# RWKV-7 state update: the decayed old state added by VectorE instead of accumulated on TensorE

## The chip, the cores and the metric

One core of a Trainium2 chip runs the whole block. Its engines are named as in the profile: PE is TensorE (PEld its weight loads), DVE VectorE, ACT ScalarE, POOL GpSimd, SP the queue of SyncE. The metric is the device time of one execution in microseconds; the time before is the median of 3 runs.

## The reference

A hybrid block on 512 tokens of width 1024: an RWKV-7 time mix beside a Conformer convolution (31 taps), a gated merge and a feed-forward part, all in float32. What the change touches is the recurrence of the time mix, for each of 16 heads with a 64 x 64 state S:

```
def step(S, inp):
    r_t, w_t, k_t, v_t, a_t, b_t = inp
    sa = einsum('bhvk,bhk->bhv', S, a_t)
    S = S * w_t[..., None, :] + sa[..., None] * b_t[..., None, :] + v_t[..., None] * k_t[..., None, :]
    y = einsum('bhvk,bhk->bhv', S, r_t)
    return S, y
```

## The kernel before

The activations lie transposed: 8 channel tiles of 128 channels (two heads each) by 512 tokens. The dense products run as three passes each on float32r halves (`acc3`: high by high, high by low, low by high); in the middle part of the program their weights are streamed by GpSimd's DMA queue (`wload`: `wh` as loaded, `wl` made by ScalarE and an accumulating second DMA).

The recurrence runs in 8 chunks of 64 tokens. For each channel tile `ct`, `prep` makes the decays and keys, `solve` inverts a unit triangular matrix per chunk on VectorE and TensorE, `values` makes the values, and `chain` (line 956) carries the state from chunk to chunk; `finish` normalises, and `taps` runs the convolution of that tile on VectorE as 31 long operations. In `chain`, each chunk `c` does this, every product into one PSUM tile `zt`:

- `zt[:, 0:2]`: the queries and keys of the chunk (`AR`) with the state `SV[c]` (line 978), copied by ScalarE to `zs` (981)
- `zt[:, 5:7]`: the inverse `pb` (the buffer `Pbd`) with `zs` (982), copied by ScalarE to `UV` (984)
- `zt[:, 3:5]`: for c > 0 the product of the unit matrix with the old state `SV[c]`, started (988), and the update, `bkT` with `UV[c]`, accumulated onto it (990)
- two ScalarE instructions, one per head, scale each half of `zt[:, 3:5]` by the decay of the chunk, `dL[:, c]`, and write it as `SV[c + 1]` (993)

```
PE.matmul(zt[:, 3:5, :], lhsT=ident, rhs=SV[:, c, :, :],
          start=True, stop=False)
PE.matmul(zt[:, 3:5, :], lhsT=bkT[:, c, :], rhs=UV[:, c, :, :],
          start=c == 0, stop=True)
```

The chains of the 8 channel tiles follow each other. Beside them TensorE works on dense tiles, VectorE on taps, the next tile's solve and the preparation of the one after, ScalarE on copies and activations. The order in which all this stands on each engine is set when the program is built: `Sched` keeps, per engine, queues of recorded instructions with estimated durations (`times`), and issues, engine by engine, the ready instruction of lowest priority number (0 for `chain`, 1 for loads, 2 for `prep` and `values`, 3 for `solve` and `finish`, 4 for dense products, 5 for `taps`). The order written in this way is fixed on the chip; an instruction that has to wait holds all that stands behind it on its engine. Recorded instructions carry the line of the helper that issues them, so nearly all rows say L300 (in `issue`) or L225 (in `call`), and are told apart by their tiles.

Of the kernel before, what the change touches and what calls it, by code (L numbers as in the profile page):

```python
# [9 lines left out]
F32 = mybir.dt.float32  # L10
F32R = mybir.dt.float32r
I32 = mybir.dt.int32
AF = mybir.ActivationFunctionType
ALU = mybir.AluOpType
# [3 lines left out]
P = 128  # L18
# [4 lines left out]
L = 64  # L23
# [58 lines left out]
def tile_hybrid_block(ctx, tc, xT, cst, prm, dwp, wl1, w2g, w_in, w_ro, w_co, w_o,  # L82
# [296 lines left out]
    V, G, S = Engine("DVE", nc.vector), Engine("POOL", nc.gpsimd), Engine("ACT", nc.scalar)  # L379
    PE, SY = Engine("PE", nc.tensor), Engine("SP", nc.sync)  # L380

    def pool(stack, name, bufs, **k):
        return Pool(stack.enter_context(tc.tile_pool(name=name, bufs=bufs, **k)), bufs)
# [5 lines left out]
    sp = pool(ctx, "sp", 2)  # L389
# [16 lines left out]
    ident = cs[:, C_ID:C_ID + P]  # L406
# [23 lines left out]
    E, O = slice(0, 64), slice(64, 128)  # L430
# [134 lines left out]
    for k in range(NT):  # L565
        if k == WK:
# [4 lines left out]
                               op0=ALU.mult, op1=ALU.subtract)  # L571
# [11 lines left out]
    def normed():  # L583
        for k in range(NT):
# [7 lines left out]
                    op0=ALU.mult, op1=ALU.add)  # L592
# [3 lines left out]
                    op0=ALU.mult, op1=ALU.add)  # L596
# [147 lines left out]
    def once(fn):  # L744
        fn()
        yield from ()
# [209 lines left out]
    def chain(ct):  # L956
        s_ = st[ct]
        if ct:
            yield ("chain", ct - 1)
        yield ("val", ct)  # L960
        yield ("solve", ct)
        AR, GR, UV, SV, pb, bkT, dL = (s_[n] for n in ("AR", "GR", "UV", "SV", "pb", "bkT", "dL"))
        yp = None

        def outputs(cs_):
            for c in cs_:
                if c > 0:
                    for par, R in ((0, E), (1, O)):
                        PE.matmul(yp[R, c, :], lhsT=SV[R, c, par, :], rhs=AR[R, c, 2, :],
                                  start=c == 1, stop=False, skip_group_check=True)  # L970
            for c in cs_:
                for par, R in ((0, E), (1, O)):
                    PE.matmul(yp[R, c, :], lhsT=UV[:, c, par, :], rhs=GR[:, c, par, :],
                              start=False, stop=True, skip_group_check=True)

        for c in range(NCH):
            zt = pc.tile([P, 7, L], F32, tag="ch", name="zt")
            PE.matmul(zt[:, 0:2, :], lhsT=AR[:, c, 0:2, :], rhs=SV[:, c, :, :],
                      start=True, stop=True)
            zs = sp.tile([P, 2, L], F32, tag="zs", name="zs")  # L980
            S.activation(out=zs, in_=zt[:, 0:2, :], func=AF.Copy)
            PE.matmul(zt[:, 5:7, :], lhsT=pb[:, c, :], rhs=zs, start=True, stop=True)
            for par, R in ((0, E), (1, O)):
                S.activation(out=UV[R, c, par, :], in_=zt[R, 5 + par, :], func=AF.Copy)
            if c < NCH - 1:

                if c > 0:
                    PE.matmul(zt[:, 3:5, :], lhsT=ident, rhs=SV[:, c, :, :],
                              start=True, stop=False)
                PE.matmul(zt[:, 3:5, :], lhsT=bkT[:, c, :], rhs=UV[:, c, :, :],  # L990
                          start=c == 0, stop=True)
                for par, R in ((0, E), (1, O)):
                    S.activation(out=SV[R, c + 1, par, :], in_=zt[R, 3 + par, :], func=AF.Identity,
                                 scale=dL[R, c:c + 1])
            if c == NCH // 2 - 1:
                yp = s_["yp"] = py.tile([P, NCH, L], F32, tag="y", name="yp")
                outputs(range(0, NCH // 2))
        outputs(range(NCH // 2, NCH))
        sc.post(("chain", ct))
        sc.spawn(once(lambda: finish(ct)), 3)  # L1000
# [130 lines left out]
    for ct in range(NT):  # L1131
        for g_, pri in ((prep, 2), (values, 2), (chain, 0), (taps, 5)):
            sc.spawn(g_(ct), pri)
# [242 lines left out]
    for h in range(2):  # L1376
        c = HALF[h]
# [83 lines left out]
```

## Time and profile before

| | before |
|---|---|
| median of 3 runs | 1114.42 us (1114.17 to 1115.25) |
| profiled execution, its own time | 1110.63 us |
| its span | 1108.9 us |
| TensorE busy | 1061.3 us (96%) |
| VectorE busy | 731.5 us (66%) |
| ScalarE busy | 568.2 us (51%) |
| GpSimd busy | 103.8 us (9%) |

The span is the time from the first to the last instruction; some 1.7 us lie around it. Busy shares are means over stages with different limits. Rows of the groups view give the busy time, the mean of one instruction in ns, and the idle time of the engine just before the group with what ended it; a row of a tile gives the minimum, median and maximum. A TensorE product of float32 tiles is recorded as two passes, so 48 products stand as 96.

### The profile page before, as it was taken

Reading aid. Unit: us, or ns where it says so; the run is one execution under the profiler, and the core shown is the slowest. Engines: PE = TensorE matmul, PEld = TensorE weight load, DVE = VectorE, ACT = ScalarE, POOL = GpSimd, SP = SyncE. Lnnn points to the kernel's source line nnn. Section 1 sums busy time; section 2 is a strip of 40 time slices with the busy share of each in tenths; the row PEclk is TensorE's granted clock in tenths of the full one; section 3 lists DMA queues with packets and bytes.
Section 4 is the critical chain, followed back from the end, with each engine's and each line's share of the span. In section 5 each row is a group of like instructions: output and inputs, shape, how many; then the busy total and the mean of one; then the engine's idle time right before and its main releaser. Section 6 shows DMA issues by size and latency. Waiting matters only on the chain.

```text
span 1108.9 us, 18596 instructions
## 1 busy us (share of the span) xinstructions
PE 1061.3 (96%) x7066; PEld 860.2 (78%) x7066; DVE 731.5 (66%) x1511; ACT 568.2 (51%) x1197; POOL 103.8 (9%) x172
## 2 busy tenths in 40 slices
PE   7799999999899999989999999999999999999996
PEld 5577787877787777768788888998888888888885
DVE  5878899899898999998553366365444444433324
ACT  5556666777777777555572235344333333323321
POOL 0003322211313222010000000000000000000000
PEclk9899999999899999999999999999999999999998
DMA  6115745434546454144232236102223222333312
GB/s 240 46 40 119 145 98 122 82 70 95 104 98 122 102 114 101 33 86 152 77 105 96 87 104 204 62 1 81 93 94 95 95 95 95 91 100 115 105 48 76
DMA packets 68872, 107.74 MB, mean 97 GB/s; under 512 B 15152, under 2 KB 20656, under 8 KB 68784
## 3 DMA queue, kind: packets, MB, share of 16 engines
q1 hardware_dynamic: 48912, 70.38, 20.2%
q0 software_dynamic: 19872, 36.18, 16.2%
q8 instruction: 56, 0.92, 0.3%
q14 instruction: 32, 0.26, 0.1%
HBM read 102.34 MB, written 2.10 MB: 94 GB/s over the span
## 4 chain that ended last, share of the span: by engine, by line
PE 83%; DVE 6%; ACT 4%; issue 1%; DMA 0%; DVEq 0%; ACTq 0%
PE dn L225 34%; PE dn L300 29%; PE zt L300 5%; PE psf L225 2%; PE wo L225 2%; PE yp L300 2%; PE gps L300 1%; ACT Mt L300 1%; PE lora L300 1%; DVE AR L300 1%; DVE GR L300 1%; DVE cacc L300 1%; DVE cpad L300 1%; PE ssy L300 1%; PE psn L225 1%
## 5 line engine op out<-in xcount | busy, mean ns | idle before, releaser
L225 ACT ACTIVATE wh<-wf 128x512 fp32r<-128x512 f32 x140 | 86.7, 619 | 219.2 <-PE dn L225 209.3
L225 DVE TENSOR_TENSOR wl<-wf,wh 128x512 fp32r<-128x512 f32 x140 | 94.4, 675 | 125.2 <-ACT wh L225 125.0
L300 PE MATMUL dn<-HH,wh 128*128 128x512 f32 x408 | 168.8, 414 | 0.0
L300 PE MATMUL dn<-HH,wl 128*128 128x512 f32 x408 | 168.1, 412 | 0.0
L300 PE MATMUL dn<-HL,wh 128*128 128x512 f32 x408 | 167.4, 410 | 0.0
L225 PE MATMUL dn<-FHL,wh 128*128 128x512 f32 x320 | 127.7, 399 | 0.0
L225 PE MATMUL dn<-FHH,wh 128*128 128x512 f32 x320 | 126.2, 394 | 0.0
L225 PE MATMUL dn<-FHH,wl 128*128 128x512 f32 x320 | 125.4, 392 | 0.0
L225 PE MATMUL dn<-FH,wh 128*128 128x512 f32 (+1 forms) x332 | 101.3, 388 | 0.0
L300 PEld LDWEIGHTS dn<-HH,wl 128*128 128x128 f32 x408 | 78.0, 191 | 14.4 <-issue 0.5
L300 PEld LDWEIGHTS dn<-HH,wh 128*128 128x128 f32 x408 | 77.8, 191 | 14.6 <-issue 0.7
L300 PEld LDWEIGHTS dn<-HL,wh 128*128 128x128 f32 x408 | 77.7, 190 | 14.6 <-issue 0.5
L300 ACT ACTIVATE wh<-wf 128x512 fp32r<-128x512 f32 x69 | 42.9, 627 | 78.5 <-PE dn L300 71.2
L300 DVE SCALAR_TENSOR_TENSOR cacc<-ca,dw,cacc 128x512 f32<-128x512 f32 x105 | 78.1, 744 | 0.0
L300 POOL DMA_DIRECT2D wl<-in_w_in_dram x69 | 60.4, 886 | 180.8 <-ACT wl L300 149.0
L300 DVE SCALAR_TENSOR_TENSOR cpad<-ca,dw,cpad 128x512 f32<-128x512 f32 x98 | 73.0, 745 | 0.1
L300 DVE TENSOR_TENSOR wl<-wf,wh 128x512 fp32r<-128x512 f32 x69 | 47.3, 688 | 38.6 <-ACT wh L300 38.6
L225 PEld LDWEIGHTS dn<-FH,wh 128*128 128x128 f32 x332 | 61.5, 188 | 13.9
L225 PEld LDWEIGHTS dn<-FHH,wh 128*128 128x128 f32 x320 | 60.1, 188 | 15.7
L225 PEld LDWEIGHTS dn<-FHH,wl 128*128 128x128 f32 x320 | 60.1, 188 | 14.3
L225 PEld LDWEIGHTS dn<-FHL,wh 128*128 128x128 f32 x320 | 60.1, 188 | 13.6
L225 PE MATMUL dn<-FH,wl 128*128 128x512 f32 (+1 forms) x166 | 64.0, 385 | 0.0
(306 smaller groups left out, 2101.6 us busy)
## 6 DMA issues: line engine op xcount, KB each, us to landing
wh<-in_w_in_dram POOLq DMA_DIRECT2D x69, 256.0 KB, 3.8
wl<-in_w_in_dram POOLq DMA_DIRECT2D x69, 256.0 KB, 4.4
wf<-in_w_gt_dram SPq DMA_DIRECT2D x44, 256.0 KB, 2.6
wf<-in_w_up_dram SPq DMA_DIRECT2D x44, 256.0 KB, 2.6
wf<-in_w_in_dram SPq DMA_DIRECT2D x43, 256.0 KB, 2.8
wf<-in_w_dn_dram SPq DMA_DIRECT2D x40, 256.0 KB, 2.7
wf<-in_w_ro_dram SPq DMA_DIRECT2D x16, 256.0 KB, 2.5
wf<-in_w_co_dram SPq DMA_DIRECT2D x16, 256.0 KB, 2.6
```

The lines of the kernel that those rows point to most:

```text
L225: return fn(*a, **k)
L300: i = fn(*a, **k)
```

## The change

The product with the unit matrix is left out. In its place, for c > 0, GpSimd multiplies each head's half of the old state with the decay into a new buffer `dS` (two in turn), and VectorE takes the update from PSUM, scales it by the same decay and adds `dS`, one instruction per head. For c = 0 the old ScalarE instructions stay.

```
             if c < NCH - 1:
 
                 if c > 0:
-                    PE.matmul(zt[:, 3:5, :], lhsT=ident, rhs=SV[:, c, :, :],
-                              start=True, stop=False)
+                    dS = sp.tile([P, L], F32, tag="dS", name="dS")
+                    for par, R in ((0, E), (1, O)):
+                        G.tensor_scalar(out=dS[R], in0=SV[R, c, par, :], scalar1=dL[R, c:c + 1],
+                                        scalar2=None, op0=ALU.mult)
                 PE.matmul(zt[:, 3:5, :], lhsT=bkT[:, c, :], rhs=UV[:, c, :, :],
-                          start=c == 0, stop=True)
+                          start=True, stop=True)
                 for par, R in ((0, E), (1, O)):
-                    S.activation(out=SV[R, c + 1, par, :], in_=zt[R, 3 + par, :], func=AF.Identity,
-                                 scale=dL[R, c:c + 1])
+                    if c > 0:
+                        V.scalar_tensor_tensor(out=SV[R, c + 1, par, :], in0=zt[R, 3 + par, :],
+                                               scalar=dL[R, c:c + 1], in1=dS[R], op0=ALU.mult,
+                                               op1=ALU.add)
+                    else:
+                        S.activation(out=SV[R, c + 1, par, :], in_=zt[R, 3 + par, :],
+                                     func=AF.Identity, scale=dL[R, c:c + 1])
```

Since `Sched` sees other instructions, it also writes another order on every engine. Three places of it follow.

TensorE, channel tile 0, before: chunk 1 from the product with the unit matrix to the first product of chunk 2 (`dn` are passes of dense tiles, `cs` holds the unit matrix).

```order
L300 MATMUL zt<-SV,cs 128x128
L300 MATMUL zt<-UV,bkT 128x128
L300 MATMUL dn<-HH,wl 128x512
L300 MATMUL dn<-HH,wh 128x512
L300 MATMUL dn<-HL,wh 128x512
L300 MATMUL dn<-HH,wl 128x512
L300 MATMUL dn<-HH,wh 128x512
L300 MATMUL dn<-HL,wh 128x512
L300 MATMUL zt<-SV,AR 128x128
```

And the same place in the changed program:

```order
L300 MATMUL zt<-UV,bkT 128x128
L300 MATMUL dn<-HH,wl 128x512
L300 MATMUL dn<-HH,wh 128x512
L300 MATMUL dn<-HL,wh 128x512
L300 MATMUL zt<-SV,AR 128x128
```

The product with the unit matrix is gone, and three dense passes instead of six stand between the update's product and the first product of the next chunk.

VectorE in the changed program, around the first update of channel tile 0 (`tt` and `Ps` belong to the solve of channel tile 1, `ca` to a convolution's input).

```order
L300 TENSOR_TENSOR tt<-Mo,Ps 128x24
L300 TENSOR_TENSOR Ps<-Ps,tt 128x2x3x4
L300 SCALAR_TENSOR_TENSOR SV<-zt,dL,dS 64x64 x2
L300 SCALAR_TENSOR_TENSOR ca<-th,dn 128x512
L300 TENSOR_TENSOR tt<-Mo,Ps 128x16
L300 TENSOR_TENSOR Ps<-Ps,tt 128x2x2x4
L300 TENSOR_TENSOR tt<-Mo,Ps 128x8
```

Before, the same operations of the solve stood here without the update. The updates of one tile's state now stand among the solve and the preparation of the following tiles, and each waits for the other in this order.

GpSimd in the changed program, at the first copies of channel tile 0.

```order
L300 DMA wh<-in_w_in_dram 128x512 x3
L300 DMA wl<-in_w_in_dram 128x512
L300 ISA
L300 TENSOR_SCALAR dS<-SV,dL 64x64 x2
L300 DMA wl<-in_w_in_dram 128x512
L300 DMA wh<-in_w_in_dram 128x512
L300 TENSOR_SCALAR dS<-SV,dL 64x64 x2
L300 DMA wl<-in_w_in_dram 128x512
L300 TENSOR_SCALAR dS<-SV,dL 64x64 x2
```

Before, only the DMA issues stood here. The copies stand between them, two per chunk, and the row ISA, a reload of GpSimd's code library, stands once, ahead of the first.

## Rows read from the trace of the kernel before

**Rows 1.** The page's head: span; busy time of each engine (share), instructions

```profile
span 1108.9 us, 18596 instructions
...
PE 1061.3 (96%) x7066; PEld 860.2 (78%) x7066; DVE 731.5 (66%) x1511; ACT 568.2 (51%) x1197; POOL 103.8 (9%) x172
```

**Rows 2.** Busy us (instructions) by stretch, then TensorE's clock, DMA share, GB/s

```profile
140.00:500.00 360.00, 342.60 (x3497) 273.53 (x3496) 329.16 (x792) 256.19 (x664) 82.10 (x130) 0.98 0.46 94
460.00:500.00 40.00, 33.71 (x268) 25.90 (x269) 37.13 (x67) 26.41 (x74) 5.22 (x6) 0.96 0.35 68
500.00:700.00 200.00, 199.07 (x874) 160.80 (x873) 113.99 (x187) 96.11 (x156) 0.00 (x0) 1.00 0.37 120
```

**Rows 3.** Who waited for whom, 140 to 500 us, PE and POOL: us, times, longest

```profile
PE zt L300 <- ACT SV L300: 3.7, 5, 0.9
PE zt L300 <- ACT zs L300: 2.6, 6, 0.6
...
POOL wl L300 <- ACT wl L300: 133.9, 26, 26.4
```

**Rows 4.** Tile `zt` (minimum/median/maximum ns), then groups by shape (busy us, mean ns)

```profile
L300 ACT ACTIVATE SV<-zt,dL x112: 291/309/312, 144.8 to 496.1; 64x64 f32<-64x64 f32 x112
...
L300 PE MATMUL zt<-SV,cs 128*128 128x128 f32 x96 | 19.9, 289 | 0.5 <-ACT UV L300 0.5
```

**Rows 5.** Timeline (start us, us), TensorE's weight loads around one unit-matrix product

```profile
304.58 0.19 PEld L300 LDWEIGHTS dn<-HH,wl 128*128 128x128 f32 x1
304.81 0.41 PEld L300 LDWEIGHTS zt<-SV,cs 128*128 128x128 f32 x2
305.14 0.30 PEld L300 LDWEIGHTS zt<-UV,bkT 128*128 128x128 f32 x2
305.37 0.19 PEld L300 LDWEIGHTS dn<-HH,wh 128*128 128x128 f32 x1
305.48 0.19 PEld L300 LDWEIGHTS dn<-HL,wh 128*128 128x128 f32 x1
```

**Rows 6.** VectorE's groups: tap, PSUM operand, short operation; then a timeline of taps

```profile
L300 DVE SCALAR_TENSOR_TENSOR cpad<-ca,dw,cpad 128x512 f32<-128x512 f32 x98 | 73.0, 745 | 0.1
...
L300 DVE TENSOR_TENSOR AR<-gps,cs 64x256 f32<-64x256 f32 x32 | 13.4, 419 | 10.3 <-ACT Mt L300 6.7 <-PE gps L300 3.3
...
L300 DVE SCALAR_TENSOR_TENSOR rw<-rt,ry 128x8 f32<-128x8 f32 x48 | 8.0, 166 | 1.5
...
281.95 0.75 DVE L300 SCALAR_TENSOR_TENSOR cacc<-ca,dw,cacc 128x512 f32<-128x512 f32 x1
282.61 0.75 DVE L300 SCALAR_TENSOR_TENSOR cpad<-ca,dw,cpad 128x512 f32<-128x512 f32 x1
```

**Rows 7.** Timeline at two updates of channel tile 0: ScalarE, then VectorE

```profile
148.54 0.62 ACT L300 ACTIVATE SV<-zt,dL 64x64 f32<-64x64 f32 x2
...
152.69 0.63 ACT L300 ACTIVATE SV<-zt,dL 64x64 f32<-64x64 f32 x2 [0.25 <-PE zt L300]
...
148.49 0.18 DVE L300 TENSOR_TENSOR Ps<-Ps,tt 128x24 f32<-128x24 f32 x1
```

**Rows 8.** GpSimd's groups (busy us, mean ns, idle before); then tile `SV`

```profile
L300 POOL DMA_DIRECT2D wl<-in_w_in_dram x69 | 60.4, 886 | 180.8 <-ACT wl L300 149.0 <-PE zt L300 13.3 <-ACT zs L300 13.1
L300 POOL DMA_DIRECT2D wh<-in_w_in_dram x69 | 41.8, 610 | 110.0 <-PE dn L300 100.1 <-PE zt L300 8.8 <-issue 0.8
...
L300 POOL MEMSET SV<- x16: 144/146/527, 67.7 to 430.1; 64x64 f32 x16
```

**Rows 9.** Tile `wl`, the streamed weights, from issue to landing

```profile
DMA to landing us min/median/max: 3.7/4.4/6.4
```

**Rows 10.** Timeline of GpSimd: ahead of the first updates, and at two memsets

```profile
145.06 0.88 POOL L300 DMA_DIRECT2D wl<-in_w_in_dram  x1 [0.20 <-issue]
...
298.55 0.90 POOL L300 DMA_DIRECT2D wl<-in_w_in_dram  x1 [0.84 <-ACT mu_v L300]
299.10 0.71 POOL L300 MEMSET SV<- 64x64 f32 x2
```

## The prediction

> **What bounds the kernel now.** I read the page's header and busy shares first, then busy time by stretch, then who waits for whom inside the stretch that the change touches, then single steps.
>
> The profiled execution took 1110.63 us (span 1108.9 and 1.7 around it). TensorE is busy 96% of the span, VectorE 66%, ScalarE 51%, GpSimd 9% [rows 1]. The state updates run from 144.8 to 496.1 us [rows 4], so the stage to look at is 140 to 500 us. There TensorE is busy 342.6 of 360 us, VectorE 329.2 (91%), ScalarE 256.2 (71%), GpSimd 82.1, and after it, to 700 us, TensorE is full but for 1 us [rows 2]. So TensorE sets the time, with VectorE close behind it. TensorE's largest waits there are a few us each: 3.7 us in 5 places for the old update on ScalarE, 2.6 us for `zs`, and none for a streamed weight [rows 3]. A microsecond of work taken off TensorE should therefore mostly come off the time, as long as no new wait takes its place. The exception is the end of the stage: from 460 to 500 us TensorE is busy 33.7 of 40 us and VectorE 37.1 [rows 2].
>
> **The unit-matrix product, removed.** There are 48 (8 channel tiles, chunks 1 to 6), recorded as 96 passes of 0.289 us mean [rows 4]. Passes overlap, so this duration is not their price; the pitch is. In the weight loads from 304.81 to 305.48 us stand two passes of this product, two of the product with `bkT`, and one dense pass; two dense loads alone stand 0.23 apart [rows 5]. So (305.48 - 304.81 - 0.23) / 4 = 0.11 us a pass, and 96 x 0.11 = 10.6 us. Six of the 48 products are those of the last channel tile, in the stretch where TensorE has idle time; I count seven eighths: **-9.3 us**, with -10.6 as the far end.
>
> **The scaled copy out of PSUM, moved from ScalarE to VectorE.** ScalarE loses 96 of its 112 `SV` instructions of 0.309 us [rows 4], some 30 us, at a place where it is 71% busy: nothing by itself. VectorE gains 96. It has no such shape now. Its fixed part is 0.166 us (128x8) and 256 columns from PSUM cost 0.419 [rows 6], so 64 columns are about 0.166 + 56 x 0.253 / 248 = 0.22 us, estimated from these two. A pair is then 0.4 to 0.45 us where ScalarE's pair spans 0.62 [rows 7]: up to 0.2 us shorter a step. TensorE waits only 3.7 us in all for that pair [rows 3], so the gain lies between 0 and 3.7 us; I take 0, for the reason that follows.
>
> **The new wait on VectorE.** The update now stands in VectorE's fixed order among the conv taps, the solve of the next channel tile and the preparation of the one after. It can find in front of it one tap of 0.745 us [rows 6], and what stands behind a late update is the next chunk's first product on TensorE, and all of TensorE's queue behind it. Ends: 0 if the dense passes between steps cover it, 48 x 0.745 = 36 us if each update meets a whole tap and nothing covers. In the changed order three dense passes (0.7 us at 0.23 each) stand between the first update's product and the next chunk's, where six stood: they cover the pair, not a tap in front of it. The nearest row is the same wait on ScalarE, whose long instructions are of much the same length: 3.7 us [rows 3]. VectorE is fuller (91% against 71%), and at 148.5 us, when ScalarE made the first such update of channel tile 0, VectorE ran the very operation of the solve (24 columns, 148.49) behind which the changed order has the update [rows 7]: planned and real pace lie close there. I take **+4 us**.
>
> **The decayed old state on GpSimd.** Two instructions of 64x64 a step, 96 in all. GpSimd has no arithmetic now; its nearest row is the memset of the same 64x64 shape, 0.146 us at the median and 0.527 at most [rows 8]. The state is ready when the update before ends (149.16) and the product is wanted when the next one starts (152.69): 3.5 us [rows 7]. Two at 0.527 behind a DMA issue of 0.886 make 1.9 us, inside that cover: 0. What is queued behind them on GpSimd are the issues of the streamed weights. GpSimd stands idle 180.8 us before the `wl` issues and 110.0 before `wh` [rows 8], and TensorE waits for no such weight now: 0. If the cover is gone (a DMA that waits in front of a copy), the update is late by that DMA's wait.
>
> **One instruction that the diff does not show.** The built program has a further GpSimd instruction in front of the first copy, a reload of GpSimd's code library, once. No row has its like. Nearest is a transfer that must land: `wl` lands 4.4 us after its issue, 6.4 at most [rows 9]. It can begin when the `wl` issue in front of it is done, 145.06 + 0.88 = 145.94, and the update is due at 148.54 [rows 7, 10]: 2.6 us are covered. Ends 0 and 6.4; 4.4 - 2.6 = 1.8, and I take **+2 us**. The Trainium skill (GPSIMD Engine Reference, 2.1 Instruction dispatch) says that the first call to a freshly loaded GpSimd kernel pays about 6 us that no profile instruction shows; with 6 in place of 4.4 this term would be 3.4 us and the sum 1.4 us more. No run here shows it yet.
>
> **Sum.** -9.3 + 4 + 2 = -3.3 us: 1107.3 on the profiled execution's 1110.63. The median of the runs shown is 1114.42, 3.8 us above that execution; the difference carried to it gives **1111.1 us**. A measurement of this kernel can tell about 0.2%, 2.2 us, from no change.
>
> **The rivals.**
> *1. GpSimd's copies take VectorE's time (slower).* VectorE is busy 329.2 of 360 us [rows 2] and gets 96 x 0.22 = 21 us more. Of the 248 conv taps, the changed order has 161 in place of 185 ahead of the last channel tile's solve, which moves 24 x 0.67 = 16 us (a tap's pitch, 282.61 - 281.95 = 0.66 [rows 6]) behind the stage. That leaves 334 us, against 342.6 - 10.6 = 332 for TensorE: two engines with one load each and a fixed order between them. If each copy also keeps VectorE from its own work for its own length, 96 x 0.146 to 0.527 = 14 to 51 us come on top. The stage has 360 us now, so it decides from 26 us, 0.27 us a copy, on; at 0.35 us it is 334 + 34 = 368, 8 us over 360; with a third of them made up in VectorE's idle time, some 5 us: about 1119 us. Against it: no row shows GpSimd and VectorE in each other's way, and the long memsets stand right behind a DMA issue [rows 10]. This is the place where a rule speaks against the change: the Trainium skill (SBUF — State Buffer, Who interferes with whom) says that a VectorE instruction with two SBUF inputs and a GpSimd instruction that reads SBUF exclude each other, the second waiting until the first is done. Taps and solve are of that kind. GpSimd's only instructions now are memsets and DMA issues, so the trace neither agrees nor disagrees. Chance 0.22.
> *2. GpSimd's queue or the reload is late (slower).* A copy that stands behind a DMA which waits, or a reload several times longer than a transfer's 4.4 us, say 13 us against 2.6 of cover: -9.3 + 4 + 10 = +5, 1119 us. For it: single waits of a `wl` issue reach 26.4 us [rows 3]. Against it: they are waits of a queue that had nothing else to do. Chance 0.12.
> *3. The new waits eat the gain (same).* Waits of 7 to 10 us in place of 6: within 2.2 us of 1114.4. The end of the stage, with little dense work left, makes this likely enough. Chance 0.20.
> *4. The wait on VectorE costs no more than the one on ScalarE did, the reload is hidden, and the pair is shorter*: -10.6 - 2: about 1102 us. Chance 0.14.
> My forecast, faster by 2.2 to 7 us, has 0.32.
>
> **How the numbers follow.** Faster by over 0.2%: 0.32 + 0.14 = 0.46. Within: 0.20. Slower: 0.34. The likeliest case alone lies between 1107 and 1112. The range takes in rival 4's most likely part and both slower rivals up to a few us over their price: 1103 to 1122, which leaves out a reload or a loss on VectorE of more than that, and the full 3.7 us shorter steps.
>
> **What would show it.** No `zt` product with the unit matrix; 96 new VectorE rows of about 0.22 us; 96 GpSimd rows of 0.15 to 0.5 us; TensorE's busy time from the first to the last update down by about 10 us. Right: TensorE's waits for `SV` on VectorE in that stage at 4 to 8 us, and one wait of a few us at the first copy. Wrong, by rival 1: taps and solve operations on VectorE longer than 0.745 and 0.18 us while a copy runs, or copies far over 0.5 us. By rival 2: VectorE's update waits mostly for GpSimd. By rival 4: TensorE's waits for `SV` under 4 us and no wait at the reload. If the time falls by more than 12 us, chunk latency and not TensorE's work was the bound, and the first step here fails.

## The result, and the profile after

Median 1122.38 us (1117.98 to 1126.00, 6 runs) against 1114.30 us (1109.82 to 1115.25, 6 runs): ratio 1.0077, 95% interval 1.0058 to 1.0096. The change costs 8.6 us. This ratio and those below leave out the few executions in a slower state, such as the one of 1715.52 us that left the only trace of t_after_no_taps. The profiled execution took 1122.0 us. That of the kernel before took 1110.63, 3.7 us under its median, so the two traces differ by more (11.3 us of span) than the medians do.

The page's head of the changed kernel (busy time, share of the span, instructions):

```profile
span 1120.2 us, 18573 instructions
...
PE 1061.0 (95%) x6970; PEld 852.5 (76%) x6970; DVE 757.0 (68%) x1600; ACT 537.7 (48%) x1101; POOL 166.1 (15%) x282
```

This pair of lines already holds the puzzle. TensorE has 96 passes less than before [rows 1], and is as long busy: 1061.0 against 1061.3 us. And it idles longer: 1120.2 - 1061.0 = 59.2 us, where it was 1108.9 - 1061.3 = 47.6. The same windows as before [rows 2] show where (TensorE, its weight loads, VectorE, ScalarE, GpSimd; then the granted clock):

```profile
140.00:500.00 360.00, 331.78 (x3324) 257.86 (x3323) 327.17 (x834) 219.24 (x551) 131.45 (x223) 0.95 0.46 93
460.00:500.00 40.00, 32.67 (x315) 25.00 (x314) 35.26 (x70) 17.62 (x50) 17.23 (x29) 0.74 0.49 95
500.00:700.00 200.00, 197.82 (x903) 159.36 (x902) 135.81 (x225) 96.88 (x162) 12.90 (x17) 1.00 0.40 121
```

In the stage TensorE idles 28.2 us (17.4 before), and its clock is 0.95 (0.98); from 460 to 500 us it is 0.74 (0.96). Who waited for whom, TensorE, 140 to 500 us, against [rows 3]:

```profile
PE zt L300 <- DVE SV L300: 11.0, 19, 1.6
PE gps L300 <- ACT Mt L300: 3.8, 6, 1.7
PE zt L300 <- ACT zs L300: 3.3, 5, 1.6
...
PE gps L300 <- ACT ys L300: 1.9, 1, 1.9
```

The wait for the state update was 3.7 us and is 11.0 (12.3 in the whole trace, in the tile's view below). `gps` holds products of the preparation of a later tile. Before, they waited:

```profile
PE gps L300 <- ACT Mt L300: 1.5, 3, 0.6
```

The view of tile `dS` (minimum/median/maximum ns; last, who waited for it: us, times):

```profile
L300 POOL TENSOR_SCALAR dS<-SV,dL x96: 432/444/1477, 146.4 to 508.0; 64x64 f32<-64x64 f32 x96
L300 DVE SCALAR_TENSOR_TENSOR SV<-zt,dL,dS x96: 239/284/293, 149.0 to 510.6; 64x64 f32<-64x64 f32 x96
...
  PE zt L300: 12.3, 22
```

The last update starts at 510.6 us, where it was 496.1 [rows 4]: the whole loss of the span has been made by then. Last, the stretches at the lower of TensorE's two clock levels (0.50 is 1.2 of 2.4 GHz) between 100 and 540 us, as windows. Before:

```profile
193.70:197.10 3.40, 3.40 (x12) 2.92 (x11) 3.31 (x7) 1.37 (x5) 2.33 (x3) 0.50 0.49 78
282.40:289.20 6.80, 6.79 (x29) 5.62 (x29) 4.52 (x13) 3.20 (x8) 1.33 (x3) 0.50 0.86 171
480.40:483.80 3.40, 3.40 (x12) 2.77 (x10) 3.40 (x6) 0.44 (x2) 0.00 (x0) 0.50 0.86 142
```

And the changed kernel:

```profile
193.70:197.10 3.40, 3.40 (x22) 2.74 (x21) 0.90 (x3) 0.84 (x3) 1.44 (x2) 0.50 0.40 90
258.60:262.00 3.40, 3.29 (x11) 2.16 (x11) 2.89 (x16) 2.34 (x6) 1.65 (x3) 0.50 0.88 145
289.30:299.50 10.20, 8.24 (x42) 6.94 (x43) 8.02 (x22) 6.54 (x17) 3.57 (x6) 0.50 0.64 105
470.20:477.00 6.80, 5.71 (x39) 4.07 (x39) 6.19 (x11) 3.36 (x11) 2.35 (x5) 0.50 0.93 233
480.40:494.10 13.70, 9.77 (x30) 7.43 (x30) 10.30 (x22) 7.17 (x20) 7.02 (x10) 0.50 0.74 115
```

37.5 us at half clock against 13.6; TensorE is busy for 30.4 and 13.6 of them. What that costs can be read from dense passes of the kernel before, two in its stretch of half clock from 282.4 us and two behind it:

```profile
288.08 0.63 PE L300 MATMUL dn<-HL,wh 128*128 128x512 f32 x1
288.51 0.63 PE L300 MATMUL dn<-HH,wl 128*128 128x512 f32 x1
...
292.13 0.40 PE L300 MATMUL dn<-HH,wl 128*128 128x512 f32 x1
292.36 0.39 PE L300 MATMUL dn<-HH,wh 128*128 128x512 f32 x1
```

They start 0.43 us apart at half clock and 0.23 at full clock. So some 46% of the busy time there is the clock's (an estimate from these rows): 14.0 and 6.3 us, 7.7 us more. That is most of the 12 us by which the busy time did not fall; the rest is not explained. The timed runs agree: their mean granted clock is 0.975 after, and 0.984 in the runs of before that stood beside the experiments. Among those runs of one and the same program, 23 at a clock of 0.987 took 1109.9 us on the mean, 20 at 0.984 took 1112.8 and 5 at 0.980 took 1115.2. At that pace the 0.009 between the two kernels goes with some 7 us. These numbers don't say which of the two, clock or idling, comes first.

### The profile page after: what moved, and what is told of

It is laid out like the page before. It is cut to its first block, busy times and chain, and to the rows that moved or that the text cites. A ratio compares the mean times of both kernels' runs of the same rounds, so it can differ in the third digit from the quotient of the medians.

```text
span 1120.2 us, 18573 instructions
## 1 busy us (share of the span) xinstructions
PE 1061.0 (95%) x6970; PEld 852.5 (76%) x6970; DVE 757.0 (68%) x1600; ACT 537.7 (48%) x1101; POOL 166.1 (15%) x282
## 4 chain that ended last, share of the span: by engine, by line
PE 71%; DVE 17%; issue 3%; ACT 2%; DMA 0%; POOL 0%; DVEq 0%; ACTq 0%; POOLq 0%
PE dn L225 34%; PE dn L300 23%; DVE cacc L300 3%; PE zt L300 2%; DVE cpad L300 2%; PE psf L225 2%; DVE SV L300 2%; PE gps L300 2%; PE wo L225 2%; DVE Ps L300 1%; DVE tt L300 1%; PE yp L300 1%; PE lora L300 1%; ACT Mt L300 1%; DVE AR L300 1%
## 5 line engine op out<-in xcount | busy, mean ns | idle before, releaser
L225 ACT ACTIVATE wh<-wf 128x512 fp32r<-128x512 f32 x140 | 86.7, 619 | 219.4 <-PE dn L225 209.3
L225 DVE TENSOR_TENSOR wl<-wf,wh 128x512 fp32r<-128x512 f32 x140 | 94.1, 674 | 125.3 <-ACT wh L225 125.2
L300 POOL DMA_DIRECT2D wl<-in_w_in_dram x76 | 66.9, 889 | 109.3 <-ACT wl L300 97.3
L225 PEld LDWEIGHTS dn<-FH,wh 128*128 128x128 f32 x332 | 61.5, 188 | 13.9
L225 PEld LDWEIGHTS dn<-FHH,wl 128*128 128x128 f32 x320 | 60.1, 188 | 15.4
L225 PEld LDWEIGHTS dn<-FHL,wh 128*128 128x128 f32 x320 | 60.1, 188 | 14.4
L225 PEld LDWEIGHTS dn<-FHH,wh 128*128 128x128 f32 x320 | 60.1, 188 | 13.8
L300 ACT ACTIVATE wh<-wf 128x512 fp32r<-128x512 f32 x62 | 38.3, 626 | 64.7 <-PE dn L300 60.1
L300 POOL TENSOR_SCALAR dS<-SV,dL 64x64 f32<-64x64 f32 x96 | 51.6, 538 | 82.5 <-DVE SV L300 62.0
```

The lines of the kernel that those rows point to most:

```text
L225: return fn(*a, **k)
L300: i = fn(*a, **k)
```

## The experiments

Two ideas were to be told apart. First: the update is late on VectorE, each step of the chain gets longer, and TensorE idles. Second: it is the order, which the planner wrote anew around it. A replanned kernel changes both at once, so some kernels below keep a written order word for word: the planner sees the old instructions, and only what it emits differs.

All of them in one table. The stage is the time from the first to the last chunk's first product (from the products of `zt` with `AR` in the trace); idle is span minus busy; half clock is its length between 100 and 540 us. These three are of the one profiled execution.

| kernel | ratio [95%] | stage us | TensorE busy / idle us | half clock us |
|---|---|---|---|---|
| before | 1 | 354.7 | 1061.3 / 47.6 | 13.6 |
| changed | 1.0077 [1.0058, 1.0096] | 369.0 | 1061.0 / 59.2 | 37.5 |
| a_no_product | 0.9875 [0.9844, 0.9906] | 341.3 | 1049.0 / 46.6 | 13.6 |
| b_vector_update | 1.0309 [1.0283, 1.0336] | 390.3 | 1078.1 / 65.5 | 51.2 |
| c_no_copies | 1.0188 [1.0162, 1.0214] | 376.1 | 1067.7 / 61.5 | 47.8 |
| g_order_no_product | 1.0002 [0.9987, 1.0017] | 354.5 | 1059.2 / 50.1 | 34.1 |
| h_change_old_order | 1.0325 [1.0294, 1.0356] | 390.1 | 1068.8 / 75.3 | 47.8 |
| c2_order_kept | 1.0054 [1.0038, 1.0070] | 362.8 | 1056.6 / 57.5 | 27.3 |
| k_scalar_new_order | 1.0038 [1.0012, 1.0063] | 365.3 | 1059.8 / 57.8 | 37.5 |
| w_vector_work | 1.0149 [1.0108, 1.0190] | 375.0 | 1068.6 / 53.9 | 37.5 |
| f_before_hold2 | 1.0175 [1.0142, 1.0209] | 358.6 | 1066.6 / 64.6 | 41.0 |
| f_after_hold2 | 1.0105 [1.0076, 1.0135] | 362.6 | 1060.0 / 60.1 | 34.1 |
| e_costs | 1.0084 [1.0054, 1.0115] | 370.6 | 1062.5 / 53.9 | 41.0 |
| p_after_reserve | 1.0152 [1.0124, 1.0180] | 376.2 | 1069.7 / 56.3 | 58.0 |
| p2_costs_reserve | 1.0120 [1.0098, 1.0142] | 373.3 | 1071.3 / 51.1 | 64.9 |
| q_before_reserve | 1.0009 [0.9989, 1.0029] | 359.9 | 1060.8 / 49.2 | 20.5 |
| t_before_no_taps | 0.9975 [0.9955, 0.9995] | 353.5 | 1060.7 / 47.2 | 13.6 |
| t_after_no_taps | 1.0025 [1.0002, 1.0047] | - | - | - |
| m_half_product | 1.0089 [1.0059, 1.0118] | 364.4 | 1071.2 / 47.4 | 27.3 |
| n_early_product | 1.0085 [1.0055, 1.0115] | 365.7 | 1066.8 / 52.7 | 30.7 |

Read its stage column against the time. From the stage's end to the span's end it is 603 to 615 us in every kernel but f_before_hold2, so the large differences are made in the stage; but a stage can also be longer because dense work that stood behind it has moved into it. The changed kernel's stage is 14.3 us longer, and the part behind it 3.2 us shorter.

Several times lie outside every range that had been given for them: those of a_no_product (13.9 us below before), b_vector_update, c_no_copies, h_change_old_order, p_after_reserve and n_early_product. Those of g_order_no_product and k_scalar_new_order lie in the range given for the second idea, the order.

The second table takes a step of the chain apart: means over chunks 1 to 5 of the eight tiles (40 steps), in us, from the starts and ends of `UV`, `zt` and `SV` in the trace.

| kernel | step | last `UV` copy to the update's product | that product to the first update | the two updates |
|---|---|---|---|---|
| before | 4.00 | 0.57 | 0.17 | 0.63 |
| a_no_product | 3.67 | 0.34 | 0.12 | 0.63 |
| changed | 4.07 | 0.34 | 0.45 | 0.60 |
| g_order_no_product | 3.97 | 0.34 | 0.30 | 0.63 |
| h_change_old_order | 4.67 | 0.34 | 0.79 | 0.78 |
| c2_order_kept | 4.00 | 0.34 | 0.41 | 0.58 |
| b_vector_update | 4.31 | 0.59 | 0.32 | 0.58 |

The removed product takes 0.57 - 0.34 = 0.23 us out of a step, and the update on VectorE puts 0.45 - 0.17 = 0.28 in. That makes the steps hardly longer, so where do 14.3 us of the stage come from? The third table splits the stage into the eight chains (from the first to the last chunk's first product) and the seven gaps between them, in us, with TensorE's idle time in each.

| kernel | chains | gaps | idle in chains | idle in gaps |
|---|---|---|---|---|
| before | 224.7 | 130.0 | 9.2 | 8.2 |
| changed | 226.7 | 142.3 | 19.0 | 10.5 |
| a_no_product | 204.1 | 137.2 | 7.8 | 9.5 |
| b_vector_update | 236.7 | 153.7 | 20.5 | 15.7 |
| g_order_no_product | 219.0 | 135.4 | 10.0 | 9.3 |
| h_change_old_order | 257.7 | 132.4 | 38.0 | 7.2 |
| k_scalar_new_order | 225.8 | 139.4 | 17.6 | 9.8 |

In the changed kernel the gaps grow, by 12.3 us, and the chains by 2.0. But its new idle time lies in the chains. Both come from the new order: besides the 96 passes of the product it takes 86 other passes out of the chains and has 97 more in the gaps. In the old order (g and h) the gaps grow by 5.4 and 2.4 us only.

### One part at a time, order written anew

**a_no_product.** Leaves out the decayed old state: its product is not made and nothing replaces it; the update stays on ScalarE.

```
-                if c > 0:
-                    PE.matmul(zt[:, 3:5, :], lhsT=ident, rhs=SV[:, c, :, :],
-                              start=True, stop=False)
                 PE.matmul(zt[:, 3:5, :], lhsT=bkT[:, c, :], rhs=UV[:, c, :, :],
-                          start=c == 0, stop=True)
+                          start=True, stop=True)
```

> The kernel before without the product with the unit matrix and with nothing in its place: the decayed old state is left out of the state update, ScalarE's two instructions stay. It prices the removed product alone. Theory 'VectorE's queue' (the product is worth what the prediction says, and the new place of the update gives it back): 8 to 12 us below the kernel before, with TensorE's waits for SV still under 5 us and the clock no lower. Rival 'nothing to gain' (TensorE is not what sets the end of this stage): within 3 us of the kernel before.

13.9 us less. The page's head:

```profile
span 1095.6 us, 18404 instructions
...
PE 1049.0 (96%) x6970; PEld 847.9 (77%) x6970; DVE 731.5 (67%) x1510; ACT 569.0 (52%) x1197; POOL 105.2 (10%) x174
```

The idle time (46.6) and the time at half clock (13.6) are as before; the gain is the 12.3 us that TensorE is less busy. In this order, which is new as well, the product is worth 12.3 us of TensorE's time.

**b_vector_update.** The product stays; only the update goes to VectorE.

```
-                    S.activation(out=SV[R, c + 1, par, :], in_=zt[R, 3 + par, :], func=AF.Identity,
-                                 scale=dL[R, c:c + 1])
+                    if c > 0:
+                        V.tensor_scalar(out=SV[R, c + 1, par, :], in0=zt[R, 3 + par, :],
+                                        scalar1=dL[R, c:c + 1], scalar2=None, op0=ALU.mult)
```

> The kernel before with the product kept; only the update for c > 0 moves from ScalarE to VectorE (one instruction per head that scales out of PSUM). No GpSimd work. Theory 'VectorE's queue': most of the loss is here, 10 to 20 us above the kernel before, TensorE waits for SV on VectorE 8 us or more. Rival 'GpSimd' (late or slow copies cost the time): within 5 us of the kernel before.

34 us more, with no GpSimd in it and no product removed. The update on VectorE, in the order that the planner wrote for it, costs more than the whole change; 23.7 us of it lie in the gaps between the chains, so not all of it is the wait for the update.

**c_no_copies.** The changed kernel without GpSimd's copies; a constant stands in for the decayed old state.

```
-                    dS = sp.tile([P, L], F32, tag="dS", name="dS")
-                    for par, R in ((0, E), (1, O)):
-                        G.tensor_scalar(out=dS[R], in0=SV[R, c, par, :], scalar1=dL[R, c:c + 1],
-                                        scalar2=None, op0=ALU.mult)
...
-                                               scalar=dL[R, c:c + 1], in1=dS[R], op0=ALU.mult,
+                                               scalar=dL[R, c:c + 1], in1=cs[R, 0:L], op0=ALU.mult,
```

> The changed kernel without GpSimd's copies: VectorE adds a constant tile in place of the decayed old state, which is left out of the computation. Theory 'VectorE's queue': within 4 us of the changed kernel, since VectorE's instructions and what stands before them are as they were. Rival 'GpSimd': the wait for the copies goes, and the time falls to that of the removed product alone, 8 us or more below the changed kernel.

Less work, and 1.1% slower than the changed kernel: the planner wrote another order. With that order kept (c2, next part) the same omission is a gain. So replanning alone is worth up to 15 us here, and one replanned kernel does not price a part.

### The written order kept

**g_order_no_product.** The order of the kernel before; the product is recorded for the planner and not emitted.

```
                 if c > 0:
-                    PE.matmul(zt[:, 3:5, :], lhsT=ident, rhs=SV[:, c, :, :],
-                              start=True, stop=False)
+                    o = PE.matmul(zt[:, 3:5, :], lhsT=ident, rhs=SV[:, c, :, :],
+                                  start=True, stop=False)
+                    o.call = []
```

> The old written order is kept word for word on every engine; only the product with the unit matrix is not emitted (the decayed old state is left out, so the output changes), the update stays on ScalarE. Left out alone and replanned it made the time 0.9875 of before (TensorE busy 12.3 us less, its idle time the same). If that gain is TensorE's work, it is here again: busy time 1049 us, ratio 0.986 to 0.991. If it came from the order that was written anew, it is gone here: 0.996 to 1.002.

No gain: 1.0002. The stage is 354.5 us long, as with the product. TensorE's work left, and TensorE then ran longer at half clock. The windows around the largest such stretch:

```profile
275.00:279.10 4.10, 2.06 (x9) 1.32 (x7) 3.96 (x7) 3.39 (x7) 1.84 (x3) 1.00 0.39 64
279.10:292.80 13.70, 13.22 (x57) 10.67 (x58) 8.59 (x24) 7.78 (x18) 2.94 (x5) 0.50 0.50 96
```

Before, the like stretch is 282.4 to 289.2 us, half as long. In both kernels TensorE is busy 4.48 of the 7 us from 275 to 282; here the idle time comes sooner (2.06 of 4.1 us busy), and the clock falls 3.3 us earlier. 34.1 us at half clock, 30.9 of them busy, cost by the 46% from above 14.2 - 6.3 = 7.9 of the 12.3 us, and the idle time grows by 2.5. That the earlier idle time is why the clock fell earlier is read from these rows, not tested.

**h_change_old_order.** The whole change in the old order: GpSimd's copies at the product's place, the update on VectorE where it stood on ScalarE.

```
+                    o.call = [("POOL", nc.gpsimd.tensor_scalar, (),
+                               dict(out=dS[R], in0=SV[R, c, par, :], scalar1=dL[R, c:c + 1],
+                                    scalar2=None, op0=ALU.mult)) for par, R in ((0, E), (1, O))]
...
+                        o.call = [("DVE", nc.vector.scalar_tensor_tensor, (),
+                                   dict(out=SV[R, c + 1, par, :], in0=zt[R, 3 + par, :],
+                                        scalar=dL[R, c:c + 1], in1=dS[R], op0=ALU.mult,
+                                        op1=ALU.add))]
```

> The whole change in the old written order: the product is not emitted, in its place in the order GpSimd makes its two copies, and where ScalarE had its update, VectorE now has it. Theory 1 (it is the place on VectorE that costs: the update stands behind a long VectorE instruction, each step gets some 0.3 us longer, TensorE idles and its clock falls): about as slow as the change, 1.002 to 1.015, time from the product's end to the update's start up from 0.17 to 0.35 us or more. Theory 2 (it is the order that was written anew): 0.987 to 0.995, the time to the update's start stays at 0.2 us.

36 us above g. TensorE's wait for the update:

```profile
PE zt L299 <- DVE SV L299: 26.9, 38, 1.8
```

So the new order does not make this wait: it brings it from 26.9 down to 11.0 us. The second idea falls in the form that the old order would have kept the gain. The new order isn't free either: it has the long gaps of the third table, and h does not have those.

**c2_order_kept.** c_no_copies in the changed kernel's own order (copies and reload not emitted).

```
-                        G.tensor_scalar(out=dS[R], in0=SV[R, c, par, :], scalar1=dL[R, c:c + 1],
-                                        scalar2=None, op0=ALU.mult)
+                        o = G.tensor_scalar(out=dS[R], in0=SV[R, c, par, :], scalar1=dL[R, c:c + 1],
+                                            scalar2=None, op0=ALU.mult)
+                        o.call = None
```

> The changed kernel with its written order kept word for word on every engine, but without GpSimd's copies and the library reload; VectorE adds a constant tile, so the decayed old state is left out of the computation. Theory 'VectorE's work' (the stage is as long as VectorE's work ahead of its end, whatever waits for what): within 3 us of the changed kernel. Rival 'GpSimd' (copies late, or VectorE kept from its work by them): 6 us or more below the changed kernel.

1.0054 against 1.0077: copies and reload together are worth some 2.6 us, which is not clear of the noise (the intervals overlap). The wait for the update stays:

```profile
PE zt L301 <- DVE SV L301: 10.9, 20, 1.5
```

**k_scalar_new_order.** The changed kernel's order without the copies, the updates emitted on ScalarE at the same point (the decayed old state is left out).

```
+                        o.call = [("ACT", nc.scalar.activation, (),
+                                   dict(out=SV[R, c + 1, par, :], in_=zt[R, 3 + par, :],
+                                        func=AF.Identity, scale=dL[R, c:c + 1]))]
```

> The written order of the changed kernel is kept; the updates are emitted on ScalarE, at the same point of the order, GpSimd's copies and the reload are not emitted (the decayed old state is left out, so the output changes). Theory 1 (VectorE's place costs): the time falls to that of the kernel without the product, 0.985 to 0.993, half-clock time back at about 14 us. Theory 2 (the new order costs): it stays at 1.000 to 1.010.

1.0038 [1.0012, 1.0063], no faster than c2 within the intervals. With every update on ScalarE, at the places of the changed order, TensorE still waits about as long as in c2:

```profile
PE zt L299 <- ACT SV L299: 10.5, 16, 1.5
```

So the engine alone is not shown to be the cause. The test is not a clean one: the update stands on an engine for which the order was not planned, and there it waits 0.28 us and the pair takes 0.73. Together with h it says that an update moved without a new plan is late on either engine, far more so on VectorE (0.79). What VectorE's place costs apart from the written order stays open.

### VectorE's load

**w_vector_work.** The kernel before with 96 more VectorE instructions of 64x64 that read the state and that nobody waits for.

```
+                    dS = sp.tile([P, L], F32, tag="dS", name="dS")
+                    for par, R in ((0, E), (1, O)):
+                        V.scalar_tensor_tensor(out=dS[R], in0=SV[R, c, par, :],
+                                               scalar=dL[R, c:c + 1], in1=SV[R, c, par, :],
+                                               op0=ALU.mult, op1=ALU.add)
```

> The kernel before with 96 more small VectorE instructions (64x64, two per chunk, from the state into a buffer that nobody reads): nobody waits for them, so no wait is added and only VectorE's work grows, by 96 x 0.2 to 0.25 us = 19 to 24 us. Theory 'VectorE's work': 15 to 28 us above the kernel before. Rival 'queue' (the changed kernel loses its time because the update waits behind taps in VectorE's order): within 5 us of the kernel before.

16.6 us for 26.4 us of work:

```profile
L300 DVE SCALAR_TENSOR_TENSOR dS<-SV,dL 64x64 f32<-64x64 f32 x96 | 26.4, 275 | 4.3 <-ACT SV L300 2.7
```

Work of chain priority on VectorE costs time even where no product waits for it. Part of it is the order written anew, which this run doesn't separate.

**f_before_hold2, f_after_hold2.** The taps of the last two channel tiles are held until the last chain is done.

```
+        if ct >= NT - 2:
+            yield ("chain", NT - 1)
         cb = conv_in[ct]
```

> The kernel before with the conv taps of the last two channel tiles held back until the last chain is done: at most 186 of the 248 taps can stand ahead of the stage's end, where 241 stood, 55 x 0.66 = 36 us of VectorE's work less; nothing else is edited. Theory 'VectorE's work': the stage shortens until TensorE's own 337 us of work bind, 8 to 18 us below the kernel before. Rival 'queue': the update is ScalarE's here, within 4 us of the kernel before. If the taps come too late for the convolution's output product, slower.

> The changed kernel with the same taps held back: 186 in place of 214 ahead of the stage's end, 18 us of VectorE's work less. Theory 'VectorE's work': 15 to 22 us below the changed kernel. Rival 'queue', in the form that only taps directly in front of an update cost: 4 to 10 us below it. Rival 'GpSimd': within 4 us of it.

From 140 to 500 us VectorE has 39 us less to do in the kernel before, and the stage is 3.9 us longer. In the changed one the stage is 6 us shorter and the time no better. In f_before_hold2 the time is lost behind the stage, in one wait:

```profile
PE bcy L300 <- ACT rxy L300: 17.5, 1, 17.5
```

**t_before_no_taps, t_after_no_taps.** Order kept, 232 of the 248 taps not emitted (the convolution is left out by that part).

```
+            if j < KW - 1 or n > 1:
+                o.call = []
```

> The same omission in the kernel before. If VectorE's load lengthens the stage only through the update, which is on ScalarE here, nothing changes: stage 350 to 356 us, ratio 0.993 to 1.002. If it lengthens the stage through the solve between the chains, the gaps between the chains (130 us) shorten and the ratio falls to 0.985 or less.

> The changed kernel in its own written order, without 232 of the 248 conv taps on VectorE (they are not emitted, so the convolution's output is wrong by that part; all else stands in the same order). If the update waits behind taps, the wait before it falls from 0.45 to 0.15 us or less, and the stage from 369 us to about 345 to 355. If it waits behind the solve and the preparation, the wait stays above 0.3 us and the stage above 360.

Before:

```profile
140.00:500.00 360.00, 343.24 (x3502) 274.27 (x3501) 198.85 (x590) 256.71 (x666) 81.80 (x130) 0.98 0.47 96
```

VectorE is busy 199 of 360 us in place of 329, and the stage is 1.2 us shorter. So VectorE's load does not bound the kernel before. The changed kernel gains 5.8 us by the same omission (1.0077 to 1.0025), the kernel before 2.8. No trace shows how much of the wait went with the taps. The changed kernel's own trace tells what stood in front: from product to update it is 21.4 us in all over 48 steps. In 18 of them VectorE was still at a tap when the product ended (8.9 us), in 27 at other work (12.2 us), and in 3 it was free. In the kernel before, ScalarE was still at work in 19 of 56, and it is 8.0 us in all.

### The planner's numbers

**e_costs** gives the planner the measured durations of the update and of the copies; **p_after_reserve** issues no other VectorE instruction that would end later than 0.35 us before a due update; **p2_costs_reserve** does both; **q_before_reserve** applies the rule to ScalarE in the kernel before.

```
+            if eng == "POOL" and name == "tensor_scalar":
+                return 0.5, 0.45, 0.0
...
+            if name == "scalar_tensor_tensor" and n == L and psum:
+                return 0.3, 0.29, 0.0
```

```
+                    if e == "DVE":
+                        due = self.due(e)
+                        heads = [h for h in heads if not h[1].pri or h[0] + h[1].busy <= due]
```

> The changed kernel with the planner's costs of the two new instructions set to what the trace shows (update on VectorE 0.30 us of its time in place of 0.146, copy on GpSimd 0.50 in place of 0.277), so that only the written order changes. Theory 'VectorE's queue', in the form that the order is at fault: taps stand further from the updates, TensorE waits less for SV, 4 to 10 us below the changed kernel. In the form that VectorE has too little time whatever the order: within 3 us of the changed kernel. Rival 'GpSimd': within 3 us too.

> The changed kernel; the planner issues no VectorE instruction of another stream that would end later than 0.35 us before the update is due, as soon as the update's product is known to be ready. Same instructions, another written order. If the wait in front of the update on VectorE is what costs (20 us in all against 9 on ScalarE before), the mean time from the product's end to the update falls from 0.45 to 0.25 us or less and the time by 5 to 12 us: ratio to before 0.997 to 1.004. If the plan and the real pace are too far apart for such a rule, the wait stays at 0.4 us and the time at 1.005 to 1.012.

> The same rule, with the planner's durations of the update and of GpSimd's copies set to those measured in the changed kernel. If the rule works and good durations help it: at or below p_after_reserve. If the written order moves the time by chance: anywhere from 1.000 to 1.012, whatever the wait does.

> The kernel before with the same rule for ScalarE. Its update waits 0.17 us on the mean there, 0.04 at the least, so at most 48 x 0.13 = 6 us are to be had: 0.995 to 1.000 if the rule works. A change by more than that, either way, would be the written order's own effect, not that of this wait.

None is faster than the changed kernel (or than before, for q). The rule did not reach its aim: in p the mean wait is 0.45 us, as without it, probably because the plan's times and the chip's are too far apart. p2 is the instructive one: least idle time of the changed kernel and its three variants here (51.1 us), a wait of 0.32 us and a step of 3.91, yet gaps of 151.4 us between the chains, 64.9 us at half clock and TensorE busy 1071.3. What it won in waits did not come off the time.

### A cheaper product

**m_half_product.** Both products of the update made per head, only the two quarters that are used.

```
+                    for par, R in ((0, E), (1, O)):
+                        PE.matmul(zt[R, 3 + par, :], lhsT=ident[R, R], rhs=SV[R, c, par, :],
+                                  start=True, stop=False, skip_group_check=True)
+                for par, R in ((0, E), (1, O)):
+                    PE.matmul(zt[R, 3 + par, :], lhsT=bkT[:, c, R], rhs=UV[:, c, par, :],
+                              start=c == 0, stop=True, skip_group_check=True)
```

> The kernel before, with the unit-matrix product and the update's product each made as one product per head, 64 columns of the stationary side and 64 of the moving side, and only the two quarters of the result that are used; the update stays on ScalarE. If the price of the product is TensorE's work by columns and rows of its tile, half or more of its 12.3 us and part of the update's product go: 0.990 to 0.996. If the small products cost as much each as the large one (or the change of tile size costs), 1.000 to 1.010.

Slower. A small pass lasts as long as a large one, and there are twice as many:

```profile
L300 PE MATMUL zt<-UV,bkT x224: 222/270/369, 145.5 to 506.3; 128*64 128x64 f32 x112
L300 PE MATMUL zt<-SV,cs x192: 218/267/366, 149.0 to 506.0; 64*64 64x64 f32 x192
L300 PE MATMUL zt<-SV,AR x128: 270/274/583, 143.1 to 507.6; 128*128 128x128 f32 x128
```

**n_early_product.** The unit-matrix product right behind the chunk's first product, ahead of the `zs` copy.

```
+            if 0 < c < NCH - 1:
+                PE.matmul(zt[:, 3:5, :], lhsT=ident, rhs=SV[:, c, :, :], start=False, stop=False,
+                          skip_group_check=True)
             zs = sp.tile([P, 2, L], F32, tag="zs", name="zs")
```

> The kernel before with the unit-matrix product recorded right behind the chunk's first product, ahead of the zs copy, so that it is done while ScalarE copies; TensorE's work is the same, the planner writes its order anew. If the 13 us that came with the product's removal were latency (0.57 us before the update's product with it, 0.34 without), they come here too, with the right output: 0.988 to 0.995. If they were TensorE's work: 0.997 to 1.005, with the step shorter or not.

The wait ahead of the update's product falls to 0.33 us, but the time from the chunk's first product to the `zs` copy rises from 0.56 to 0.87: the step is as long as before (4.06 us), and the kernel slower. The product's 0.2 to 0.3 us lie on the step's path wherever it stands there. No version here that computes the whole block beats the kernel before.

## Why the prediction was wrong

The forecast was 1111.1 us, faster; the measured 1122.38 is slower and lies 0.4 us above the range. That its upper end comes so near is luck: it stood for other mechanisms, a late reload or copies in VectorE's way. On the two spans: -12.3 us of the product's work, +12.0 us of TensorE's busy time that came back, +11.6 us of idle time: 11.3 us, the difference of the two spans.

- **The product's work** (-9.3, far end -10.6): 12.3 us, by a_no_product. The size was nearly right. What failed is the sentence that carries it to the time, that a microsecond taken off TensorE "should therefore mostly come off the time". In the old order nothing came off (g: 1.0002): time at half clock (7.9 us) and idle time (2.5 us) took the place of the work. A busy share of 96% was read as a bound; left out was that the pace of the work and the idle time can change with it.
- **The clock** was in no term and in no rival. Half clock grew from 13.6 to 37.5 us; the busy part of that is worth 7.7 of the 12.0 us. The signs stood in the trace of before: it too falls to half clock for 6.8 us at 282.4, after TensorE had been busy only 4.48 of the 7 us before 282. That idling there makes the clock fall is read from rows; no run here set the clock by itself.
- **The wait on VectorE** (+4, ends 0 and 36) is the term that was mis-sized. TensorE waits 12.3 us for the update against 3.7, and 5.7 us for `Mt` and `ys` ahead of `gps` against 1.5: 12.8 us more in all, about the 11.6 by which its idle time grew. The forecast took its size from the same wait on ScalarE. But a pair is 0.60 us, not 0.40 to 0.45, and VectorE was still at work ahead of 45 of 48 updates, ScalarE ahead of 19 of 56: 91% busy should have counted for the far end. What the forecast says of the dense passes held: from the update's product to the next chunk's first they keep TensorE busy 0.95 us a step (0.90 before), which covers the pair and not a long operation in front of it. The argument that the planned and the real pace lie close at 148.5 us held at that one update: there it follows the solve's operation at once (148.98). On the mean the update came 0.45 us behind its product. The whole price of the move differs with the written order: 34 us by b, 36 by h over g, 2.0% (1.0077/0.9875) by the changed kernel over a, but only some 4 us by the changed kernel over k, copies included.
- **GpSimd** (+2 for the reload, 0 for the copies): about 2.6 us together by c2. A copy has 0.444 us at the median, inside the bounds of 0.146 to 0.527, but 1.477 at most. No wait is seen at the reload; the timeline of GpSimd at the first copies, against [rows 10]:

```profile
145.35 0.88 POOL L300 DMA_DIRECT2D wl<-in_w_in_dram  x1 [0.21 <-issue]
146.38 0.98 POOL L300 TENSOR_SCALAR dS<-SV,dL 64x64 f32<-64x64 f32 x2
147.41 0.91 POOL L300 DMA_DIRECT2D wl<-in_w_in_dram  x1
```

  The first copy starts 0.15 us after the issue in front of it ended, and the pair takes 0.98 us, like the next one at 149.35. The 6 us that the Trainium skill (GPSIMD Engine Reference, 2.1 Instruction dispatch) gives for a first call are not there.
- **Rival 1**, GpSimd in VectorE's way, came near the time (1119 us), but its mechanism is not what happened. On the mean the taps are as long as before [rows 6]:

```profile
L300 DVE SCALAR_TENSOR_TENSOR cacc<-ca,dw,cacc 128x512 f32<-128x512 f32 x105 | 78.3, 746 | 0.3
L300 DVE SCALAR_TENSOR_TENSOR cpad<-ca,dw,cpad 128x512 f32<-128x512 f32 x98 | 73.2, 747 | 0.2
```

  The copies are what gets longer. One pair in GpSimd's timeline (start us, us):

```profile
460.01 1.32 POOL L300 TENSOR_SCALAR dS<-SV,dL 64x64 f32<-64x64 f32 x2 [3.06 <-DVE SV L300]
```

  And VectorE's timeline beside it:

```profile
459.95 0.29 DVE L300 SCALAR_TENSOR_TENSOR SV<-zt,dL,dS 64x64 f32<-64x64 f32 x1
460.27 0.75 DVE L300 SCALAR_TENSOR_TENSOR cacc<-ca,dw,cacc 128x512 f32<-128x512 f32 x1
460.94 0.81 DVE L300 SCALAR_TENSOR_TENSOR cpad<-ca,dw,cpad 128x512 f32<-128x512 f32 x1
```

  1.32 us beside taps, 0.98 beside the short operations of the solve at 146.38. The 27 copies that overlap a tap take 0.65 us on the mean, the others 0.50. The tap at 460.94, which starts while such a copy runs, takes 0.81 us in place of 0.75; 11 of the 233 taps take 0.80 or more, none did before, and that is under 1 us in all. So the sign is there, but nearly all of the waiting is GpSimd's, whose copies have the time. This fits the rule of the Trainium skill (SBUF — State Buffer, Who interferes with whom) that one of the two waits for the other.
- **Rival 2** fell: VectorE's update waits for TensorE's product, not for GpSimd; in c2, without the copies, it is as late (0.41 us).

Open: why two orders of the same instructions have 37.5 and 58.0 us of half clock (the changed kernel and p_after_reserve), what part of a_no_product's gain is its order (with the old order the gain isn't there), and what part of the change's loss is the order with its longer gaps and not the update's place on VectorE (in k the wait is as long).

## What to carry to other kernels

A busy share of 96% is no proof that taking work off an engine shortens the time: take the work out with the written order kept, and see whether the stage gets shorter. A step of a serial chain belongs where it finds nothing long in front of it. Pricing its move by the wait of a similar step on another engine gave 4 us for some 9 of direct wait, and the time that goes with the move was anything from 4 to 36 us with the written order. So when a planner writes the order anew, split the stage into the chains and the gaps between them before a loss is put down to the step that was edited. In these traces the stretches of half clock follow TensorE's idling; where that is so, count a new wait twice, once as idle time and once as slower work behind it.

## What was not expected of the hardware

- Half clock took back most of what TensorE was spared: in g_order_no_product, 96 passes less and 20.5 us more at half clock, at an unchanged time.
- A 64x64 pass with 64 columns took 267 ns at the median, one of 128x128 with 128 columns 274.
- GpSimd's multiplication of 64x64 took 0.444 us at the median where its memset of the same shape takes 0.146 [rows 8].
